# A retention head's key scaling, states and outputs moved 12 to 14 steps later behind the pair of products they come from

## The chip, the cores and the metric

One core of one Trainium2 chip runs the program. The metric is the device time of one execution in microseconds. The median of three runs before the change is 1666.28 us (1666.15 to 1666.56).

## What is computed

One layer of a streaming encoder over 512 frames of 2048 channels: a norm, one large projection, two mixers whose outputs are gated and merged, an output projection, and a gated addition. The change lies in mixer B, a retention of eight heads in chunks, cut here to its core:

```python
scores = einsum('bnqhd,bnkhd->bnhqk', qc, kc) * intra_decay
intra = einsum('bnhqk,bnkhe->bnqhe', scores, vc)
kv = einsum('bnkhd,bnkhe->nbhde', kc * to_end, vc)
def step(state, kv_c):
    return state * chunk_decay + kv_c, state
_, prev = lax.scan(step, zeros, kv)
cross = einsum('bnqhd,nbhde->bnqhe', qc * from_start, prev)
y = intra + cross      # then a GroupNorm per head
```

qc and kc are the rotated queries and keys of a head, vc its values. The kernel works in chunks of 128 frames, so a head has four blocks of queries and three states.

## The kernel before

All large products are written as pairs: `gemm_pair` (L255) makes two blocks of 128 output channels from seven products of half size (a Strassen scheme), in four PSUM banks p, v, q and r. Each weight is split into a high half wh, made on ACT (L156), and a low rest wl, made on DVE (L161); L163 and an accumulating transfer on POOL (L119) form the sums of weights. The seven products n = 0 to 6 are run in 14 runs of eight matmuls: 0h, 1h, 0l, 1l, 2h, 3h, 2l, 3l, 4l, 4h, 5h, 5l, 6l, 6h (h with wh, l with wl). They stand in the trace as L326, with the names ps_v for n = 0 and 5, ps_p for 1, 4 and 6, ps_q for 2 and ps_r for 3. After some runs results are taken out of PSUM: ACT copies one (L265), DVE combines two (L269, e_t) and adds halves (L1117, go).

The order of the instructions on each engine is written out by hand. `step()` is called after every second matmul of a pair, 56 times a pair, and advances a count. `later(n, f)` puts f in line to be recorded n steps on. What f does is then recorded at that place in the order of its engines, and each engine works through its own order; between engines there are semaphores.

The part around the change is the loop over the eight heads (L1130): for each head one pair that makes its queries and keys (`u_r`), then two pairs of gate channels (`u_g`). When a gate half is complete, `to` (L1124) makes its sigmoid on ACT (L1126, go<-go) and ACT issues its store (L1127). I call the two pairs behind a head's own its first and second gate pair; all of the head's further work is recorded between their matmuls.

That work is in `retention(h)` (L896). Queries and keys are rotated (`rotate`, L907). Counted from the rotation of the keys, which is one step into the first gate pair, a table (L1013 to L1017) says at which step each part is recorded:

- `queries` (L919): the queries times their factor, qt, on DVE.
- `keys(0)` to `keys(2)`: the keys are transposed in 32x32 blocks on DVE (kb, L940), sent to DRAM by four transfers (L948) and loaded back turned as kr (L958), all transfers on SP.
- `keys(3)`: ACT scales kr to kn (L961).
- `scores` and `decay`: ps_rs on PE (L928), at on DVE (L932).
- `states`: ps_kv on PE (L969, weights kn), then the states on ACT (L972) and DVE (L975).
- `values_out`: seven products ps_y on PE (L984, L986) from at, qt and the states.
- `norm`, `scale`, `back`: statistics, scaling and turning of the outputs on DVE and POOL (L991 to L1003, L940), sent to DRAM as yb.

Beside this a top-k step is recorded on DVE now and then (L776, L777, with rows of 256, 384 or 512 scores), one in each 40 steps, by a background queue.

Of the kernel before, what the change touches and what calls it, by code (L numbers as in the profile page):

```python
# [21 lines left out]
NT = L // 128  # L22
# [13 lines left out]
def block_kernel(tc, xT, pT, posb, posq, w_in, w_v, w_r0, w_r1, w_ik, w_a, w_b, w_o, w_ple, w_gate,  # L36
# [4 lines left out]
    with contextlib.ExitStack() as ctx:  # L41
# [10 lines left out]
        def U(name, dt=F32):  # L52
            return up.tile([128, L], dt, name=name, tag="u")

        def B(name, dt=F32):
            return bp.tile([128, 1280], dt, name=name, tag="b")

        def P(name):
            return pp.tile([128, L], F32, name=name, tag="p")

        def S(name, n):
            return sm.tile([128, n], F32, name=name, tag=f"s{n}")

        def tok(t):
            return slice(128 * t, 128 * t + 128)
# [381 lines left out]
        for k in range(KT):  # L447
            if k in (1, 2, 3, 4, 5, 7, 9, 11, 13, 15):
                load_to(state["raw"] + 1)
            if k < 10:  # L450
                t = U("xk")
                sp.dma_start(t, xT[:, k, :])
                xs.append(t)
            elif k % 2 == 0:
                t = B("xk2")
# [440 lines left out]
        def retention(h):  # L896
# [38 lines left out]
            def turn(src, n, name):  # L935


                b = U(name)
                w = 32 * n
                dve.transpose(out=b[:, 0:4 * w].rearrange("p (j t c) -> p t j c", j=4, t=n),  # L940
                              in_=src[:, 0:4 * w].rearrange("p (t j c) -> p t j c", t=n, j=4))
                return b[:, 0:4 * w]

            def send(b, dst):

                w = b.shape[1] // 4
                for i in range(4):
                    sp.dma_start(dst.rearrange("(j r) (i x) -> i r j x", j=4, i=4)[i],  # L948
                                 b[32 * i:32 * i + 32, :].rearrange("r (j x) -> r j x", j=4))

            def keys(i):
                if i == 0:
                    E["kb"] = turn(E[1], 3, "kb")
                elif i == 1:
                    send(E["kb"], krd[h])
                elif i == 2:
                    E["kr"] = U("kr")
                    sp.dma_start(E["kr"][:, 0:384], krd[h])  # L958
                else:
                    E["kn"] = U("kn")  # L960
                    act.activation(E["kn"][:, 0:384].rearrange("p (t i c) -> p i t c", t=3, i=4),  # L961
                                   E["kr"][:, 0:384].rearrange("p (i t c) -> p i t c", i=4, t=3),
                                   AF.Copy, scale=dect[:, 256:257])

            def states(i):
                if i == 0:
                    ps = E["ps"] = P("ps_kv")
                    for t in range(3):
                        pe.matmul(ps[:, tok(t)], E["kn"][:, tok(t)], rv[:, tok(t)], start=True, stop=True)  # L969
                elif i == 1:  # L970
                    E["s"] = U("state")
                    act.activation(E["s"][:, 0:128], E["ps"][:, 0:128], AF.Copy)  # L972
                else:
                    for t in (1, 2):
                        dve.scalar_tensor_tensor(E["s"][:, tok(t)], E["s"][:, tok(t - 1)], g128, E["ps"][:, tok(t)],  # L975
                                                 op0=OP.mult, op1=OP.add)

            def values_out(t):
                if t == 0:
                    E["py"] = P("ps_y")  # L980
                    E["st"] = S("gst", 24)
                    E["mv"] = S("gmv", 8)
                o = E["py"][:, tok(t)]
                pe.matmul(o, E["at"][:, tok(t)], rv[:, tok(t)], start=True, stop=(t == 0))  # L984
                if t:
                    pe.matmul(o, E["qt"][:, tok(t - 1)], E["s"][:, tok(t - 1)], start=False, stop=True)  # L986
# [20 lines left out]
            def back(i):  # L1007
                if i == 0:
                    E["yb"] = turn(E["yn"], NT, "yb")
                else:  # L1010
                    send(E["yb"], yd[h])

            steps = [(9, queries), (11, lambda: keys(0)), (21, lambda: keys(1)), (29, lambda: keys(2))]  # L1013
            steps += [(24, scores), (28, decay), (36, lambda: keys(3))]
            steps += [(n, lambda i=i: states(i)) for i, n in enumerate((41, 43, 45))]
            steps += [(53, lambda t=t: values_out(t)) for t in range(NT)]
            steps += [(59, norm), (70, scale), (74, lambda: back(0)), (84, lambda: back(1))]  # L1017
            return rotate

        x_wanted = collections.deque(x_away)  # L1020
# [109 lines left out]
        for h in range(NH):  # L1130
            if state["rate"] == BG_RATES[2]:
                later(38, lambda: hold(True))
                later(64, lambda: hold(False))
            gate_pair(u_r[h], retention(h))
            for n in (2 * h, 2 * h + 1):
                d, m = ((sgb, 2 * n), (sga, 2 * n - 16))[n >= 8]
                gate_pair(u_g[n], to(d[m:m + 2], AF.Sigmoid))
# [187 lines left out]
        for m in PAIRED:  # L1325
            t = B("sm")
# [18 lines left out]
        for m in range(8):  # L1345
# [13 lines left out]
            if m == 7:  # L1359
                todo.extend([None] * 24)  # L1360
                for k in range(2):
                    t = U("pk")
# [14 lines left out]
        for m in range(MF):  # L1377
            i = u_p[m // 4][0]
# [12 lines left out]
            t = U("pw")  # L1391
# [360 lines left out]
```

## Time and profile before

| what | value |
|---|---|
| median of three runs | 1666.28 us |
| the profiled execution's own time | 1665.03 us |
| its span, first to last instruction | 1663.2 us |
| PE (matmuls) busy | 1643.0 us, 99% of the span |
| DVE busy | 1313.7 us, 79% |
| ACT busy | 963.3 us, 58% |
| POOL busy | 233.0 us, 14% |
| chain that ended last | PE 87%, DVE 6%, ACT 3%, DMA 3%, issue 1% |

PE is matmuls, PEld the loading of their weights, SP the engine that issues most transfers. The retention heads run from about 280 to 770 us. In a timeline each line is a start, a duration, the engine, the line of the kernel, the operation, what it writes <- what it reads, the shape and a count; in brackets stands how long the engine had been idle before it and what released it. An engine's idle time costs something only where PE comes to wait for it. The matmuls are of 32-bit type and show as two instructions each where both halves of an operand are 32 bits wide (ps_kv: three products, six instructions).

### The profile page before, as it was taken

To read this page: it belongs to the slowest core of one execution; us is meant where nothing else is said; L and a number is where in the kernel's file an instruction comes from. 1 tells how busy PE (TensorE), PEld (TensorE's weight loads), DVE (VectorE), ACT (ScalarE), POOL (GpSimd) and SP (SyncE) were. 2 spreads that over 40 slices of the span, in tenths; PEclk is the share of its full clock that TensorE was granted. 3 is DMA by queue.
4 is the path that set the end of the run, shared out by engine and by line. 5 is a ranking of instruction groups with operands and counts; after the bars stand their busy time and mean duration, and the time that the engine had idled before them with its cause. 6 is when DMAs were issued, how large, how long until landed. Compare 5 with 4: busy or idle time off the path is not lost.

```text
span 1663.2 us, 25259 instructions
## 1 busy us (share of the span) xinstructions
PE 1643.0 (99%) x9278; PEld 1442.4 (87%) x9278; DVE 1313.7 (79%) x2038; ACT 963.3 (58%) x1481; POOL 233.0 (14%) x257
## 2 busy tenths in 40 slices
PE   9999999999999999999999999999999999999998
PEld 8988888888888888888888888888888888888997
DVE  8788879878988888877766766687768877888884
ACT  6556545555555555666877766566643544576653
POOL 3100111111111112112331122100000111100112
PEclk9999999999999999999999999999999999999999
DMA  8327999788788788788998888998566688765973
GB/s 314 111 87 238 325 258 270 191 215 220 194 217 222 193 207 222 175 229 240 254 245 223 214 231 219 241 370 283 184 206 193 182 213 220 207 218 149 245 229 143
DMA packets 138747, 365.84 MB, mean 220 GB/s; under 512 B 20672, under 2 KB 34496, under 8 KB 138624
## 3 DMA queue, kind: packets, MB, share of 16 engines
q1 hardware_dynamic: 98368, 242.92, 42.6%
q0 software_dynamic: 27440, 98.32, 31.7%
q10 hardware_dynamic: 12816, 23.00, 3.8%
q8 instruction: 73, 1.20, 0.3%
q14 instruction: 50, 0.41, 0.1%
HBM read 314.89 MB, written 49.28 MB: 219 GB/s over the span
## 4 chain that ended last, share of the span: by engine, by line
PE 87%; DVE 6%; ACT 3%; DMA 3%; issue 1%; SPq 0%; DVEq 0%; ACTq 0%
PE ps_p L326 23%; PE ps_v L326 15%; PE ps_q L326 8%; PE ps_r L326 7%; PE ps_w L233 3%; PE ps_w L232 3%; PE ps_w L234 3%; PE ps_vn L881 2%; PE ps_vn L880 2%; PE ps_vn L879 2%; DMA kr<-krd 2%; PE ps_iq L234 1%; PE ps_iq L232 1%; PE ps_iq L233 1%; DVE wl L161 1%
## 5 line engine op out<-in xcount | busy, mean ns | idle before, releaser
L161 DVE TENSOR_TENSOR wl<-wraw,wh 128x1024 fp32r<-128x1024 f32 (+3 forms) x472 | 568.1, 1216 | 160.1 <-ACT wh L156 158.1
L156 ACT ACTIVATE wh<-wraw 128x1024 fp32r<-128x1024 f32 (+3 forms) x471 | 485.9, 1041 | 241.8 <-DVE wraw L163 116.6
L119 POOL DMA_DIRECT2D wraw<-w_in x120 | 106.5, 963 | 583.6 <-DVE wl L161 343.0
L326 PE MATMUL ps_p<-hs,wh 128*128 128x512 f32 x640 | 162.4, 393 | 0.0
L265 ACT ACTIVATE e<-ps_p 128x512 f32<-128x512 f32 x152 | 90.2, 594 | 114.7 <-PE ps_p L326 113.9
L326 PEld LDWEIGHTS ps_p<-hs,wh 128*128 128x128 f32 x640 | 114.5, 189 | 19.9
L326 PE MATMUL ps_p<-hs,wl 128*128 128x256 f32 x640 | 90.2, 284 | 0.0
L326 PEld LDWEIGHTS ps_p<-hs,wl 128*128 128x128 f32 x640 | 82.5, 192 | 0.5
L326 PE MATMUL ps_v<-ha,wh 128*128 128x512 f32 x320 | 81.1, 392 | 0.0
L326 PE MATMUL ps_q<-ha,wh 128*128 128x512 f32 x320 | 80.7, 394 | 0.0
L326 PE MATMUL ps_v<-hs,wh 128*128 128x512 f32 x320 | 79.1, 389 | 0.0
L326 PE MATMUL ps_r<-hs,wh 128*128 128x512 f32 x320 | 79.0, 389 | 0.0
L326 PE MATMUL ps_p<-ha,wh 128*128 128x512 f32 x320 | 79.0, 389 | 0.0
L800 ACT ACTIVATE mk<-relf,thr 128x512 f16<-128x512 f32 (+3 forms) x128 | 66.6, 554 | 16.5 <-DVE go L1117 12.0
L1117 DVE TENSOR_TENSOR go<-e_t 128x256 f32<-128x256 f32 x160 | 68.2, 426 | 5.7
L326 PEld LDWEIGHTS ps_v<-hs,wh 128*128 128x128 f32 x320 | 60.1, 188 | 12.7
L326 PEld LDWEIGHTS ps_r<-hs,wh 128*128 128x128 f32 x320 | 60.1, 188 | 12.5
L326 PEld LDWEIGHTS ps_p<-ha,wh 128*128 128x128 f32 x320 | 60.1, 188 | 12.5
L119 POOL DMA_DIRECT2D wraw<-w_o x24 | 21.1, 942 | 348.5 <-DVE t L356 191.5
L326 PEld LDWEIGHTS ps_v<-ha,wh 128*128 128x128 f32 x320 | 59.5, 188 | 11.9
L269 DVE TENSOR_TENSOR e_t<-ps_p,pv 128x512 f32<-128x512 f32 x48 | 33.1, 690 | 46.0 <-ACT e L265 45.9
L326 PEld LDWEIGHTS ps_q<-ha,wh 128*128 128x128 f32 x320 | 57.5, 189 | 12.1 <-issue 1.7
(478 smaller groups left out, 3807.4 us busy)
## 6 DMA issues: line engine op xcount, KB each, us to landing
wraw<-w_in SPq DMA_DIRECT2D x170, 512.0 KB, 5.3
wraw<-w_in POOLq DMA_DIRECT2D x120, 512.0 KB, 8.0
wraw<-w_o SPq DMA_DIRECT2D x32, 512.0 KB, 5.0
wraw<-w_o POOLq DMA_DIRECT2D x24, 512.0 KB, 6.7
wraw<-w_gate SPq DMA_DIRECT2D x24, 512.0 KB, 5.1
wraw<-w_v SPq DMA_DIRECT2D x16, 512.0 KB, 9.2
wraw<-w_b SPq DMA_DIRECT2D x16, 512.0 KB, 5.7
wraw<-w_a SPq DMA_DIRECT2D x16, 512.0 KB, 4.2
```

What stands on the lines that cost most here:

```text
L119: pool.dma_start(out=view(raw_tiles[r], nk, cols), in_=src[:, k0:k0 + nk, :], accum_op=OP.add)
L156: act.activation(h, raw, AF.Copy)
L161: dve.tensor_sub(l, raw, h.bitcast(F32))
L232: pe.matmul(o, h[:, k, w], a, start=(s == order[0]), stop=False)
L233: pe.matmul(o, h[:, k, w], b, start=False, stop=False)
L234: pe.matmul(o, l[:, k, w], a, start=False, stop=(s == order[-1]))
L265: act.activation(E[n], src, AF.Copy)
L326: pe.matmul(o[:, co], w[:, k], src, start=(n < 4 and begin and k == 0 and j == 0), stop=(ended[n] == 16), skip_group_check=True)
L800: act.activation(bias_e[b][i // per][:, ln * (i % per):ln * (i % per + 1)], relf[:, :ln], AF.Sign, bias=thr[:, q:q + 1])
L879: pe.matmul(o, a[:, tok(t)], h[:, k], start=(s == 0), stop=False)
L880: pe.matmul(o, a[:, tok(t)], l[:, k], start=False, stop=False)
L1117: dve.tensor_add(o[:, q], c0, c1)
```

## The change

Only the table of steps is changed. `queries` goes from step 9 to 44, `keys(1)` from 21 to 20, `keys(2)` from 29 to 27, `keys(3)` from 36 to 50, the three `states` from 41, 43, 45 to 53, 55, 57, `values_out` from 53 to 66, `norm` from 59 to 72, `scale` from 70 to 83, `back` from 74 and 84 to 87 and 97. `keys(0)`, `scores` and `decay` stay. What is computed stays the same.

```diff
--- before.py
+++ after.py
@@ -1010,11 +1010,11 @@
                 else:
                     send(E["yb"], yd[h])
 
-            steps = [(9, queries), (11, lambda: keys(0)), (21, lambda: keys(1)), (29, lambda: keys(2))]
-            steps += [(24, scores), (28, decay), (36, lambda: keys(3))]
-            steps += [(n, lambda i=i: states(i)) for i, n in enumerate((41, 43, 45))]
-            steps += [(53, lambda t=t: values_out(t)) for t in range(NT)]
-            steps += [(59, norm), (70, scale), (74, lambda: back(0)), (84, lambda: back(1))]
+            steps = [(11, lambda: keys(0)), (20, lambda: keys(1)), (27, lambda: keys(2))]
+            steps += [(24, scores), (28, decay), (44, queries), (50, lambda: keys(3))]
+            steps += [(n, lambda i=i: states(i)) for i, n in enumerate((53, 55, 57))]
+            steps += [(66, lambda t=t: values_out(t)) for t in range(NT)]
+            steps += [(72, norm), (83, scale), (87, lambda: back(0)), (97, lambda: back(1))]
             return rotate
 
         x_wanted = collections.deque(x_away)
```

**ACT, the second head's first gate pair, before.** wh is the high half of a weight, e a copy out of PSUM, kn the scaled keys, go<-go a gate half's sigmoid, the DMA its store.

```order
L156 ACTIVATE wh<-wraw 128x1024 x3
L961 ACTIVATE kn<-kr,dect 128x4x3x32
L265 ACTIVATE e_3728<-ps_p 128x512
L156 ACTIVATE wh<-wraw 128x1024
L972 ACTIVATE state<-ps_kv 128x128
L156 ACTIVATE wh<-wraw 128x1024
L1126 ACTIVATE go<-go 128x512
L1127 DMA sgb<-go 128x512
```

The scaled keys come behind three wh, ahead of the copy e, of two more wh and of the sigmoid.

**ACT, the same place, after.**

```order
L156 ACTIVATE wh<-wraw 128x1024 x3
L265 ACTIVATE e_3724<-ps_p 128x512
L156 ACTIVATE wh<-wraw 128x1024 x2
L1126 ACTIVATE go<-go 128x512
L1127 DMA sgb<-go 128x512
L961 ACTIVATE kn<-kr,dect 128x4x3x32
L972 ACTIVATE state<-ps_kv 128x128
L265 ACTIVATE e_3783<-ps_p 128x512
```

kn has moved behind the copy, both wh, the sigmoid and the issue of its store; `state` now follows it directly.

**DVE, the same pair from the transposed keys on, before.** kb is the transposed keys, wl a weight's low rest, m and isc a top-k step, e_t and go<-e_t the taking out of a product.

```order
L921 TENSOR_TENSOR qt<-go,dect 128x384
L940 STREAM_TRANSPOSE kb<-go 128x3x4x32
L161 TENSOR_TENSOR wl<-wraw,wh 128x1024 x2
L163 TENSOR_TENSOR wraw<-wraw 128x1024
L269 TENSOR_TENSOR e_t<-ps_q,e_3640 128x512
L1117 TENSOR_TENSOR go<-e_t 128x256
L932 TENSOR_TENSOR at<-ps_rs,dect 128x512
...
L161 TENSOR_TENSOR wl<-wraw,wh 128x1024 x2
L975 SCALAR_TENSOR_TENSOR state<-state,ps_kv 128x128 x2
L269 TENSOR_TENSOR e_t<-ps_v,e_3728 128x512
L1117 TENSOR_TENSOR go<-e_t 128x256
```

qt stands right ahead of kb, and the two state updates right ahead of the e_t that reads ps_v.

**DVE, the same place, after.**

```order
L940 STREAM_TRANSPOSE kb<-go 128x3x4x32
...
L161 TENSOR_TENSOR wl<-wraw,wh 128x1024 x2
L921 TENSOR_TENSOR qt<-go,dect 128x384
L269 TENSOR_TENSOR e_t<-ps_v,e_3724 128x512
L1117 TENSOR_TENSOR go<-e_t 128x256
L161 TENSOR_TENSOR wl<-wraw,wh 128x1024
L269 TENSOR_TENSOR e_t<-ps_p,pv 128x512
L1117 TENSOR_TENSOR go<-e_t 128x256
L269 TENSOR_TENSOR e_t<-ps_r,e_3783 128x512
L1117 TENSOR_TENSOR go<-e_t 128x256
L161 TENSOR_TENSOR wl<-wraw,wh 128x1024
L975 SCALAR_TENSOR_TENSOR state<-state,ps_kv 128x128 x2
```

qt now stands between the last wl and that e_t; the state updates have gone behind the pair's last go and the next wl.

## Rows read from the trace of the kernel before

**Rows 1.** The page, part 4: the chain that ended last, by engine and line.
```profile
PE 87%; DVE 6%; ACT 3%; DMA 3%; issue 1%; SPq 0%; DVEq 0%; ACTq 0%
PE ps_p L326 23%; PE ps_v L326 15%; PE ps_q L326 8%; PE ps_r L326 7%; PE ps_w L233 3%; PE ps_w L232 3%; PE ps_w L234 3%; PE ps_vn L881 2%; PE ps_vn L880 2%; PE ps_vn L879 2%; DMA kr<-krd 2%; PE ps_iq L234 1%; PE ps_iq L232 1%; PE ps_iq L233 1%; DVE wl L161 1%
```

**Rows 2.** The waits: engine, line, what for; us in total, times, longest.
```profile
PEld ps_kv L969 <- ACT kn L961: 14.6, 8, 3.0
...
ACT kn L961 <- DMA kr<-krd: 12.6, 7, 2.6
...
PE ps_kv L969 <- ACT kn L961: 11.2, 7, 2.6
```

**Rows 3.** The timeline of the second head's first gate pair.
```profile
347.46 1.98 PE L326 MATMUL ps_v<-hs,wh 128*128 128x512 f32 x8
...
354.79 0.69 DVE L776 MAX8 m<-isc 128x8 f32<-128x512 f32 x1
...
356.19 0.55 DVE L921 TENSOR_TENSOR qt<-go,dect 128x384 f32<-128x384 f32 x1
...
356.65 0.57 DVE L940 STREAM_TRANSPOSE kb<-go 128x384 f32<-128x384 f32 x1
...
362.30 1.21 DVE L161 TENSOR_TENSOR wl<-wraw,wh 128x1024 fp32r<-128x1024 f32 x1
...
362.41 1.07 PE L326 MATMUL ps_v<-ha,wh 128*128 128x512 f32 x4
...
363.44 0.42 DVE L776 MAX8 m<-isc 128x8 f32<-128x256 f32 x1
...
364.29 1.22 DVE L161 TENSOR_TENSOR wl<-wraw,wh 128x1024 fp32r<-128x1024 f32 x1
...
365.41 0.61 ACT L961 ACTIVATE kn<-kr,dect 128x384 f32<-128x384 f32 x1 [2.56 <-DMA kr<-krd]
...
366.08 0.94 PE L969 MATMUL ps_kv<-rvh,kn 128*128 128x128 f32 x6 [2.60 <-ACT kn L961]
...
367.49 1.23 DVE L161 TENSOR_TENSOR wl<-wraw,wh 128x1024 fp32r<-128x1024 f32 x1 [1.98 <-ACT wh L156]
```

**Rows 4.** The timeline of PE, third head's first gate pair.
```profile
412.05 1.75 PE L326 MATMUL ps_v<-hs,wh 128*128 128x512 f32 x7
...
426.84 1.07 PE L326 MATMUL ps_v<-ha,wh 128*128 128x512 f32 x4
```

**Rows 5.** The timeline of a pair without retention work ahead of its end.
```profile
387.01 1.98 PE L326 MATMUL ps_v<-ha,wh 128*128 128x512 f32 x8
...
388.79 1.23 DVE L161 TENSOR_TENSOR wl<-wraw,wh 128x1024 fp32r<-128x1024 f32 x1 [0.35 <-ACT wh L156]
...
388.82 1.12 PE L326 MATMUL ps_v<-ha,wl 128*128 128x256 f32 x8
...
389.98 0.69 DVE L269 TENSOR_TENSOR e_t<-ps_v,e 128x512 f32<-128x512 f32 x1
...
390.74 2.00 PE L326 MATMUL ps_p<-hs,wh 128*128 128x512 f32 x8
...
391.16 0.63 ACT L1126 ACTIVATE go<-go 128x512 f32<-128x512 f32 x1 [1.08 <-DVE go L1117]
```

**Rows 6.** The timeline at the start of the second head's second gate pair.
```profile
373.09 1.99 PE L326 MATMUL ps_v<-hs,wh 128*128 128x512 f32 x8
...
373.93 0.69 DVE L269 TENSOR_TENSOR e_t<-ps_p,pv 128x512 f32<-128x512 f32 x1 [2.49 <-ACT e L265]
...
376.17 0.63 ACT L1126 ACTIVATE go<-go 128x512 f32<-128x512 f32 x1 [1.33 <-DVE go L1117]
...
377.26 1.06 ACT L156 ACTIVATE wh<-wraw 128x1024 fp32r<-128x1024 f32 x1 [0.46 <-ACT go L1126]
```

**Rows 7.** The tile qt: count, duration ns min/median/max, first and last start.
```profile
L921 DVE TENSOR_TENSOR qt<-go,dect x8: 546/549/552, 292.6 to 736.2; 128x384 f32<-128x384 f32 x8
```

**Rows 8.** The windows: busy us and count of PE, PEld, DVE, ACT, POOL, then clock, DMA.
```profile
275.00:760.00 485.00, 473.61 (x2787) 418.29 (x2786) 411.39 (x646) 267.70 (x348) 76.17 (x79) 1.00 0.83 211
```

## Prediction

> **What bounds the kernel now.** I read the page's chain first. PE carries 87% of it, and the one link that is not arithmetic and comes again and again is the load kr<-krd, 2% of the span [rows 1]. The waits say where PE stands still: past the start it is nearly all in one place, ps_kv (L969) waiting for kn (L961) on ACT, 11.2 us in seven of the eight heads as PE's matmuls count it and 14.6 us in eight as its weight loads do. Behind that stands ACT waiting for kr, 12.6 us [rows 2].
>
> The timeline of the second head's first gate pair (start 347.46) shows the mechanism. I name a pair's runs of eight matmuls by product and half: 4h, 5h (ps_v<-ha,wh at 362.41), 5l (the same product with wl), 6l, 6h (ps_p<-hs,wh). ACT comes to kn 2.56 us before kr has landed, starts it at 365.41, and ps_kv follows at 366.08, 0.67 later. A wh that is due on ACT stands behind kn, and DVE, which needs it, idles for 1.98 us until 367.49 [rows 3]. So the wait stops three engines, and DVE leaves it with nothing queued when 5l ends.
>
> What PE loses by pace: in this head 5h starts 14.95 us into the pair, in the third head 14.79 (426.84 less 412.05), the usual figure [rows 3, 4]. The 0.16 is a run held for a late wl; I count it with the loss. Half of 5h is 0.91 (half of 388.82 less 387.01, in a pair without retention, [rows 5]), so ps_kv was due at 15.70 and came at 18.62: 2.92 lost. Done so for the eight heads: 1.6, 2.9, 0.9, 0.4, 1.9, 2.1, 3.0, 0.7, together **13.4 us**, between the two figures of the waits. That is all the change can win.
>
> **The change, part by part.** *keys(3) from 36 to 50, states(0) from 41 to 53.* ps_kv moves from the middle of 5h to the middle of 6h, 3.73 us of matmuls (390.74 less 387.01, [rows 5]), and kn goes with it. kr lands 2.56 us after today's turn of kn, so the wait for kr is over. But kn now stands on ACT behind the sigmoid of the gate's first half and the issue of its store (L1126, L1127), in every head. That sigmoid waits for go (L1117) on DVE, that for e_t (L269), and that for the end of 5l on PE. A new chain ends at ps_kv, and PE comes to it soon after 5l.
>
> When PE gets there: 3.73 + 0.91 = 4.64 after the start of 5h, 19.43 into the pair.
>
> When kn is ready: e_t to the sigmoid takes 1.18 (389.98 to 391.16, [rows 5]); from a sigmoid to the next instruction behind its store 1.09 (376.17 to 377.26, [rows 6]); kn to ps_kv 0.67 [rows 3]. So ps_kv starts 2.94 after e_t does, and PE waits wherever e_t starts later than 16.49 into the pair. It can't start that early: 5l, which it reads, ends 2.93 after 5h starts (387.01 to the end of the run at 388.82), at 17.72 [rows 5].
>
> When e_t starts. Two things hold it. (a) ACT, which copies the end of 4h and then makes the wh for the last wl ahead of e_t: that wl starts 1.78 after 5h does (387.01 to 388.79, [rows 5]). A wl takes 1.14 to its successor (362.30 to 363.44), and qt, which the change puts right behind it, 0.46 (356.19 to 356.65, [rows 3]). So e_t is not before 14.79 + 1.78 + 1.14 + 0.46 = 18.17, and the wait not under **1.68 us** a head. (b) DVE itself. Its stream has no gap from kb to the wl at 364.29, and today's pause of 1.98 behind that goes, for the wh it waited on no longer stands behind kn. With qt gone from ahead of it, kb starts where qt does now, 356.19, and all of it moves 0.46 forward [rows 3]: wl at 363.83, the next at 364.97, qt 366.11, e_t 366.57. Sigmoid 367.75, kn 368.84, ps_kv **369.51**; PE is there at 347.46 + 19.43 = 366.89. It waits **2.6 us**, against 2.9 now.
>
> The same count for the other heads: from kb to e_t lie 9.53 us of DVE work (366.57 less 356.19, less 0.85 for the top-k step from 363.44 to 364.29) and whatever top-k step falls between; the longest takes 1.40 (354.79 to 356.19), the middle one 1.13 [rows 3]. kb would start at 8.45, 8.73, 8.18, 7.31, 8.18, 8.44, 9.15 and 7.31 into the pairs, which is where qt starts now: the first of the eight at 292.6 in a pair from 284.19, the last at 736.2 in one from 728.85 [rows 7]. With top-k steps of 1.40, 0.85, 1.13, 1.40, 1.13, 1.40, none, none this puts e_t at 19.4, 19.1, 18.8, 18.2, 19.3, 19.4, 19.1, 18.2; in the fifth head the step comes behind the wl that (a) holds, in the seventh ACT has a mask more to make, 0.9 late, in the eighth (a) alone decides. The waits are 2.9, 2.6, 2.3, 1.7, 2.8, 2.9, 2.5, 1.7, together **19.4 us**.
>
> *queries from 9 to 44.* Counted above: 0.46 earlier for kb, and so for kr, and 0.46 more ahead of e_t. Its reader is values_out, 22 steps later.
>
> *keys(1), keys(2) one and two steps earlier.* The rows of SP and of POOL stand in the same order before and after, so no transfer passes another. Zero; cover: kr is there at 365.41 now and wanted at 368.84.
>
> *values_out from 53 to 66.* The same matmuls, now in the next pair. They need the states, which DVE makes behind two e_t, two go and one wl of that pair. The first of these e_t starts 0.84 into a pair (373.09 to 373.93, [rows 6]), the five take about 3.3, the two state updates 0.6: ready near 4.8. PE reaches the first product at about 4.4 and the one that needs the second update some 1.2 later. Zero, with 0.8 of cover.
>
> *norm, scale, back 13 steps later.* No matmul of this stage reads them. The products leave the first gate pair and lengthen the second by about 1.5 us, so DVE gets room where it gets work. Zero.
>
> **The sum.** 19.4 - 13.4 = 6.0 us more. The profiled execution took 1665.03, so it would take 1671.0; the median shown is 1.25 above it: **1672.2 us**. Lower end: were DVE always free when 5l ends, e_t would start 0.04 behind it, as at 389.98; PE would be at ps_kv 1.67 later (391.65) and kn's product 2.94 later, so 1.27 a head and 10.1 in all [rows 5], 3.3 less than now: 1663.0. Upper end: if another 0.6 (the time of two state updates) gathered on DVE or ACT in each head, 4.8 more: 1677.0. I take the count by DVE's own stream, since its rows show no gap that could absorb it.
>
> **Rivals.** *DVE keeps up* (0.13). The point that decides is e_t's start, at or near the end of 5l. For it: in pairs without retention it is so [rows 5]. Against: those have no qt, kb or at ahead of it. 1663 to 1669, no change that can be told.
>
> *The wait is gone* (0.07): kr's landing was the whole of it, all 13.4 us come back, and the time is 1652.9, faster. It decides if kn is done 4.6 us after 5h starts. For it: before kn ACT waits for kr alone now [rows 2]. Against: kn's place on ACT behind the sigmoid, and that nothing ran past a waiting kn on ACT, the wh least of all [rows 3].
>
> *A second wait, at ps_y or for loads* (0.10). The cover of 0.8 above is thin, and the later store of yb holds SP's queue, behind which weight loads stand. With another 1 us a head the time is 1680.
>
> *The clock falls* (0.03). The granted clock is 1.00, the level of 2.4 GHz, over the whole stage [rows 8], waits of up to 3.0 us at the weight loads included [rows 2]; the longest that I forecast is no longer. If it fell, PE's work behind ps_kv to the end of the next pair's first run, about 3.4 us, would take twice as long in eight heads: 1699. The Trainium skill, "TensorE: Matmul & The Clock Gate", Part 1, says that a TensorE left idle goes back to 1.2 GHz; by that rule a stall that grows at this place costs more than itself. The trace so far shows no stall that did it.
>
> **How the numbers follow.** My forecast has 0.67. Runs of this kernel can tell 0.2%, 3.3 us, from no change. Slower by more: most of my own case (0.62), the second wait and the clock, 0.75. Within: the rest of mine and most of the first rival, 0.16. Faster: the wait gone and the lowest end of the first rival, 0.09. The range 1666.0 to 1678.0 holds my case, the upper part of the first rival and the nearer part of the second wait.
>
> **What would show it.** In the changed kernel's profile ACT's wait for kr at L961 should be gone, and L1126, waiting for go, should stand right ahead of kn in time; PE's wait at ps_kv should be 16 to 21 us by the pace, in the middle of 6h, with e_t (L269, reading ps_v) starting 18 to 19.5 us into each first gate pair; DVE's pause before the last wl should be gone. I am wrong if kn starts within 1 us of the end of 5l, or if e_t does.

## The result and the profile after

The changed kernel takes 1686.88 us, median of five runs (1684.96 to 1689.56), against 1666.28 before: ratio 1.0119, 95% interval 1.0101 to 1.0137. That is 20.6 us slower where 6 were forecast, and above the range. (The 1666.28 is also the median of five runs of the kernel before, which go from 1665.19 to 1670.87.)

In the profiled execution (1689.56 us, span 1687.4) the page's chain no longer helps: its shares add up to 61%, and the load kr<-krd of [rows 1] is not among its lines.

```profile
PE 54%; DVE 3%; ACT 2%; issue 1%; DMA 1%; DVEq 0%; ACTq 0%
```

So I go to the waits of the changed kernel, over the retention heads alone (280 to 780 us): engine, line, what for; us in total, times, longest.

```profile
ACT wh L156 <- DMA wraw<-w_in: 23.2, 16, 3.4
...
PE ps_kv L969 <- ACT kn L961: 19.0, 8, 3.3
...
ACT kn L961 <- ACT go L1126: 3.8, 8, 0.7
...
PEld ps_r L326 <- ACT wh L156: 3.3, 7, 1.2
...
PEld ps_p L326 <- DVE wl L161: 2.3, 4, 1.0
```

Three things are read here against [rows 2]. kn's wait for kr is gone, and in its place kn waits for the sigmoid L1126, in all eight heads. ps_kv waits for kn more than before, 19.0 against 11.2. And there are small waits of PE for weights, with ACT waiting 23.2 us for their loads; the same row before reads 3.5 (shown in experiment 2).

The timeline of the second head's first gate pair, which starts at 349.81, answers to [rows 3]:

```profile
369.65 0.55 DVE L921 TENSOR_TENSOR qt<-go,dect 128x384 f32<-128x384 f32 x1
...
370.12 0.68 DVE L269 TENSOR_TENSOR e_t<-ps_v,e 128x512 f32<-128x512 f32 x1
370.84 0.42 DVE L1117 TENSOR_TENSOR go<-e_t 128x256 f32<-128x256 f32 x1
...
371.30 0.63 ACT L1126 ACTIVATE go<-go 128x512 f32<-128x512 f32 x1 [2.72 <-DVE go L1117]
371.96 0.33 ACTq L1127 DMA_DIRECT2D sgb<-go  x1
372.39 0.61 ACT L961 ACTIVATE kn<-kr,dect 128x384 f32<-128x384 f32 x1 [0.46 <-ACT go L1126]
...
373.06 0.94 PE L969 MATMUL ps_kv<-rvh,kn 128*128 128x128 f32 x6 [2.19 <-ACT kn L961]
...
373.75 1.41 PE L326 MATMUL ps_p<-hs,wh 128*128 128x512 f32 x4
...
374.96 3.38 PE L326 MATMUL ps_v<-hs,wh 128*128 128x512 f32 x8
...
378.17 2.00 PE L326 MATMUL ps_p<-ha,wh 128*128 128x512 f32 x8
```

The chain is the forecast one: qt, e_t, go, the sigmoid, its store, kn, ps_kv, and 2.94 us from e_t (370.12) to ps_kv (373.06), to the hundredth. But the row at 374.96 is new: the eight matmuls of the next pair's first run take 3.38 us, where the same run takes 1.98 in [rows 3]. The windows show why (us of the window, busy us and count of PE, PEld, DVE, ACT, POOL, then the granted clock, DMA's share, GB/s):

```profile
371.00:374.50 3.50, 1.44 (x9) 1.34 (x10) 1.40 (x2) 1.52 (x3) 1.72 (x3) 1.00 0.83 178
374.50:377.92 3.42, 3.42 (x9) 2.67 (x8) 2.02 (x4) 1.55 (x2) 0.07 (x1) 0.50 0.95 202
377.92:381.33 3.41, 3.41 (x22) 3.02 (x21) 1.74 (x4) 1.69 (x2) 0.00 (x0) 1.00 1.04 211
...
275.00:780.00 505.00, 482.43 (x2759) 421.26 (x2759) 407.42 (x634) 266.88 (x345) 75.07 (x78) 0.98 0.79 201
```

From 374.50 to 377.92 the granted clock is 0.50, the 1.2 GHz level, and PE gets 9 instructions done where the next stretch of the same length, with shorter matmuls among its own, holds 22. Such a stretch, 3.41 us long each time, follows the wait at ps_kv in six of the eight heads: at 306.24, 374.50, 439.36, 572.48, 640.74 and 709.01. The profiled execution before has none ahead of the last 5 us. [Rows 8] said 1.00 over the stage; now it is 0.98.

**Where the 24.2 us between the two spans went** (1687.4 less 1663.2):

- The wait at ps_kv by the pace: 2.8, 2.4, 2.4, 2.0, 3.0, 3.4, 2.4, 1.9 in the eight heads, 20.3 together against 13.4: 6.9.
- Late weights: PE comes later to the middle of 6h in the first gate pairs, by 5.7 us in the eight together, and three of the heads' own pairs take 20.69, 20.72 and 19.93 instead of 19.64 (from a pair's first matmul to the end of its last), 2.4: together 8.1.
- That leaves 9.2 for the six stretches at half the clock, of which each can cost up to 1.7 (half of 3.41). The rows agree. From ps_kv to the next pair's second run it is 5.11 us in the second head (373.06 to 378.17) and 3.54 in the fourth, where the clock stays at 1.00:

```profile
505.37 0.94 PE L969 MATMUL ps_kv<-rvh,kn 128*128 128x128 f32 x6 [1.88 <-ACT kn L961]
...
508.91 1.98 PE L326 MATMUL ps_p<-ha,wh 128*128 128x512 f32 x8
```

Over the heads it is 5.05 to 5.12 in the six with such a stretch and 3.54 to 3.55 in the other two: 1.6 for each fall, 9.4 for six.

### The profile page after: what moved, and what is told of

It reads as the page before. It is cut to its first block, busy times and chain, and to the rows that moved or that the text cites. A ratio compares the mean times of both kernels' runs of the same rounds, so it can differ in the third digit from the quotient of the medians.

```text
span 1687.4 us, 25266 instructions
## 1 busy us (share of the span) xinstructions
PE 1656.0 (98%) x9278; PEld 1448.9 (86%) x9278; DVE 1313.3 (78%) x2038; ACT 964.4 (57%) x1481; POOL 233.4 (14%) x257
## 4 chain that ended last, share of the span: by engine, by line
PE 54%; DVE 3%; ACT 2%; issue 1%; DMA 1%; DVEq 0%; ACTq 0%
PE ps_p L326 16%; PE ps_v L326 10%; PE ps_q L326 5%; PE ps_r L326 5%; PE ps_w L232 3%; PE ps_w L233 3%; PE ps_w L234 3%; PE ps_pg L234 1%; PE ps_pg L232 1%; PE ps_pg L233 1%; DMA wraw<-w_in 1%; PE ps_pg L1536 1%; PE ps_pg L1538 1%; PE ps_pg L1537 1%; PE ps_bias L813 1%
## 5 line engine op out<-in xcount | busy, mean ns | idle before, releaser
L119 POOL DMA_DIRECT2D wraw<-w_in x120 | 106.1, 945 | 563.4 <-DVE wl L161 424.7
L326 PE MATMUL ps_v<-hs,wh 128*128 128x512 f32 x320 | 84.7, 410 | 0.0
L326 PEld LDWEIGHTS ps_v<-hs,wh 128*128 128x128 f32 x320 | 65.0, 203 | 14.5
L119 POOL DMA_DIRECT2D wraw<-w_o x24 | 21.1, 939 | 348.6 <-DVE t L356 191.5
```

The lines of the kernel that those rows point to most:

```text
L119: pool.dma_start(out=view(raw_tiles[r], nk, cols), in_=src[:, k0:k0 + nk, :], accum_op=OP.add)
L326: pe.matmul(o[:, co], w[:, k], src, start=(n < 4 and begin and k == 0 and j == 0), stop=(ended[n] == 16), skip_group_check=True)
```

## The experiments

My theory then: three separate costs, the wait at ps_kv, falls of the clock that this idle time of PE brings, and weights that come late because yb's store holds SP's queue. The main rivals: the falls have a cause of their own; the weights are late because DVE and ACT have more to do. All times are medians; each run's kernel before was measured beside it, and its median was 1668.16, 1670.33 and 1668.19 in the three groups (experiments 1 to 4, 5 to 7, 8 and 9). The changed kernel was not measured again beside them, so "less than the changed kernel" compares across groups. Counted from each group's own kernel before, the same gains are 2 to 4 us larger: 28.9, 10.2, 9.1, 36.1 and 10.7 in experiments 1, 2, 3, 4 and 6.

**1. The keys' scaling ahead of the sigmoid.**

```diff
-            steps += [(24, scores), (28, decay), (44, queries), (50, lambda: keys(3))]
+            steps += [(24, scores), (28, decay), (44, queries), (45, lambda: keys(3))]
```

> The changed kernel with one part altered: keys(3) at step 45, so that kn stands on ACT between the last two wh of the pair, ahead of the sigmoid (L1126) and its store; states stay in the middle of 6h. Theory (kn's place behind the sigmoid makes the wait at ps_kv, and the idle PE there makes the clock fall): the 20 us of wait by pace go nearly to zero, no stretch of granted clock 0.5 after ps_kv, so 10 us of falls go too; the late weights stay (about 7 us): 1660, at most 1664. Rival A (the falls have another cause than the wait): the falls stay, about 1667 to 1670. Rival B (kr lands so late that kn waits again, now holding a wh): a wait for kr of over 1 us a head at kn, 1670 or more.

Measured: 1659.89 us (1658.65 to 1661.87), ratio to before 0.9949 (0.9930 to 0.9967), 27.0 less than the changed kernel. The same place of its timeline, in the pair that starts at 345.32:

```profile
364.44 0.62 ACT L961 ACTIVATE kn<-kr,dect 128x384 f32<-128x384 f32 x1 [1.51 <-DMA kr<-krd]
...
365.69 0.68 DVE L269 TENSOR_TENSOR e_t<-ps_v,e 128x512 f32<-128x512 f32 x1
...
366.27 0.83 PE L969 MATMUL ps_kv<-rvh,kn 128*128 128x128 f32 x6
...
366.87 0.63 ACT L1126 ACTIVATE go<-go 128x512 f32<-128x512 f32 x1 [0.86 <-DVE go L1117]
```

ps_kv has no bracket: PE does not wait. kn still waits 1.51 for kr, in four heads 4.0 us together, and PE has work all the while. No stretch at 0.50 is left ahead of the kernel's last 5 us. The wait and the falls go together, which excludes rival A; the late weights stay (PE's weight loads wait 3.8 us for wh at ps_r).

**2. The store of yb behind the loads.**

```diff
-            steps += [(72, norm), (83, scale), (87, lambda: back(0)), (97, lambda: back(1))]
+            steps += [(72, norm), (83, scale), (87, lambda: back(0)), (112, lambda: back(1))]
```

> The changed kernel with one part altered: back(1), with the store of yb, at step 112 instead of 97, so that on SP's queue the store stands behind the loads of the next weights. Theory (the store, which becomes ready later than before at the same place of SP's queue, holds the loads of wraw behind it; so wh and wl come late): SP's wait for yb falls from 57 us to under 25, PE's small waits for wh and wl (some 5 us at ps_r, ps_p, ps_v) shrink below 1.5, own pairs of a head take 19.7 again instead of 20.7; time 1679 to 1682. Waits at ps_kv and the clock's falls stay. Rival (weights are late because DVE and ACT have more to do there, not for SP): no change, 1685 to 1689, and the time from landing to wh grows instead.

Measured: 1678.57 us (1677.33 to 1680.46), ratio 1.0062 (1.0041 to 1.0083), 8.3 less than the changed kernel. back(1) is the four stores and nothing else; on SP one load of wraw moves ahead of them. The rows of SP, POOL and ACT around the own pair of the fifth head show what that does. The kernel before, pair from 517.18:

```profile
509.66 1.78 SPq L948 DMA_DIRECT2D yd<-yb  x4
511.48 1.81 SPq L132 DMA_DIRECT2D wraw<-w_in  x3
...
515.60 0.92 POOL L119 DMA_DIRECT2D wraw<-w_in  x1 [10.39 <-DVE wl L161]
...
523.44 1.06 ACT L156 ACTIVATE wh<-wraw 128x1024 fp32r<-128x1024 f32 x1
```

The changed kernel, pair from 528.13:

```profile
522.58 1.78 SPq L948 DMA_DIRECT2D yd<-yb  x4
524.40 1.41 SPq L132 DMA_DIRECT2D wraw<-w_in  x3
...
526.33 0.92 POOL L119 DMA_DIRECT2D wraw<-w_in  x1 [8.23 <-DVE wl L161]
...
537.35 1.06 ACT L156 ACTIVATE wh<-wraw 128x1024 fp32r<-128x1024 f32 x1 [2.88 <-DMA wraw<-w_in]
...
539.72 1.21 PE L326 MATMUL ps_p<-hs,wl 128*128 128x256 f32 x8 [0.33 <-DVE wl L161]
```

This experiment, pair from 521.73:

```profile
508.35 4.07 SPq L132 DMA_DIRECT2D wraw<-w_in  x2
516.18 1.77 SPq L948 DMA_DIRECT2D yd<-yb  x4
518.05 0.88 SPq L132 DMA_DIRECT2D wraw<-w_in  x2
...
519.93 0.92 POOL L119 DMA_DIRECT2D wraw<-w_in  x1 [8.23 <-DVE wl L161]
...
529.14 1.06 ACT L156 ACTIVATE wh<-wraw 128x1024 fp32r<-128x1024 f32 x1 [1.07 <-DMA wraw<-w_in]
```

Counted from the start of the pair, the stores came at -7.52 before and at -5.55 after, and the three loads behind them at -5.70 and -3.73. The third wh of the pair came at 6.26 before and at 9.22 after, where ACT waits 2.88 us for a load. With one load let ahead of the stores it comes at 7.41, and the pair takes 19.64 again.

The transfer that this wh waits for is none of SP's three. It is POOL's accumulating one (L119), the row between, which is issued no later than before: 1.58 us ahead of the pair before, 1.80 ahead in both kernels after. It takes longer to land, and wh starts when it lands. In KB and us from issue to landing, before, in the changed kernel and here:

```profile
wraw<-w_in POOLq DMA_DIRECT2D x1, 512.0 KB, 7.8
```
```profile
wraw<-w_in POOLq DMA_DIRECT2D x1, 512.0 KB, 11.0
```
```profile
wraw<-w_in POOLq DMA_DIRECT2D x1, 512.0 KB, 9.2
```

In the seven own pairs of the stage the first of these transfers has medians of 8.4, 10.5 and 9.2, and in the changed kernel 14 of the 16 waits, 22.3 of the 23.2 us, end with one of POOL. So the loads behind the store, issued 2 us later, come close ahead of POOL's transfer: the first of them 4.12 us ahead of it before, 1.93 in the changed kernel with three loads, 1.88 here with two. While POOL's transfer is in flight the DMA share is 1.02, 1.01 and 0.99, so that it shares full engines with them fits; no run moves POOL's transfers alone. The totals of the stage agree. Before, the changed kernel and this one:

```profile
ACT wh L156 <- DMA wraw<-w_in: 3.5, 5, 1.2
...
SPq L948 <- DVE yb L940: 28.0, 6, 5.1
```
```profile
SPq L948 <- DVE yb L940: 57.1, 7, 8.9
```
```profile
ACT wh L156 <- DMA wraw<-w_in: 8.7, 8, 2.4
...
SPq L948 <- DVE yb L940: 32.9, 8, 5.1
```

The wait for yb was to fall under 25 and is 32.9: the two kernels after are 57.1 and 32.9, in the expected direction, and PE's small waits, as its weight loads count them, go from 8.4 to 1.5. The time is 0.4 under the expected range. The falls were to stay, and the profiled execution has three instead of six; but the four runs' mean clock, 0.993 to 0.996, is that of the changed kernel's five, 0.992 to 0.996, so the falls don't explain the 8.3. DVE's and ACT's work was left where it was, so in the changed kernel most of it is the store's place. What is left of the late weights lies in the sixth and seventh heads, where PE comes to 6h 0.4 and 1.2 late and kb starts 1.0 and 1.1 later than counted.

This run also tests the count of the wait without the late weights. e_t starts 19.34, 19.09, 18.81, 18.34, 19.31, 20.38, 20.10 and 18.18 us into the eight first gate pairs, within 0.15 of the forecast in six of them, and the waits at ps_kv are 19.4 together by the pace, as forecast.

**3. Fill for the idle time.**

```diff
                     ps = E["ps"] = P("ps_kv")
+                    for n in range(6):
+                        pe.matmul(ps, identr, Xh["s3"][0], start=True, stop=True)
```

> The changed kernel with six more matmuls of 128x512 in each head, written into ps_kv's own bank right ahead of its three products and overwritten by them: 1.4 us of PE work a head into a wait of 1.9 to 3.4 us. Theory (PE standing still at ps_kv is what makes the clock fall): the wait left at ps_kv is 0.5 to 2 us a head, the six falls go, nothing else moves: 1676 to 1680, about 8 less although PE has 11 us more to do. Rival A (the clock falls for another reason, such as the load of the chip over the whole stage): falls stay in five or six heads, time 1685 to 1689. Rival B (the fills delay ps_kv since the wait is not real slack): 1690 to 1698.

Measured: 1679.66 us (1677.48 to 1681.71), ratio 1.0067 (1.0046 to 1.0088): 7.2 less than the changed kernel, with 48 matmuls more to do. The waits, and the only stretch at 0.50 in the stage with the stretch ahead of it:

```profile
PE ps_kv L971 <- ACT kn L961: 7.8, 8, 1.9
```
```profile
629.75:633.16 3.42, 1.55 (x9) 1.03 (x8) 2.07 (x3) 1.24 (x2) 1.62 (x3) 1.00 0.64 114
633.16:636.58 3.42, 3.42 (x11) 2.74 (x10) 0.63 (x1) 1.53 (x3) 0.85 (x1) 0.50 1.06 239
```

ps_kv's idle time goes from 19.0 to 7.8 us, the falls from six to one, and the mean granted clock of the runs from 0.992 to 0.996 up to 0.997 to 0.999. The load of the chip was not lowered, the idle time was. Rivals A and B are both out. The remaining fall is in the sixth head, which had the longest wait. Between the two profiled executions, each the slowest of its kernel's runs, lie 7.9 us and five falls: again 1.6 each, if nothing else differs.

**4. Both alterations, 1 and 2.**

> The changed kernel with both alterations: keys(3) at 45 and back(1) at 112. Theory (wait at ps_kv with the falls, and late weights by SP's queue, are the two causes and independent): 1653 to 1658, faster than the kernel before by 8 or more, PE waits in the eight heads under 5 us together. Rival (they share a cause, so the two gains don't add): 1660 or more.

Measured: 1652.71 us (1652.32 to 1654.12), ratio 0.9907 (0.9888 to 0.9927): faster than the kernel before by 15 us. The gains of 1 and 2 add nearly: 27.0 and 8.3 make 35.3, measured 34.2 (from the group's own kernel before, 39.1 and 36.1). The time is 0.3 under the expected range. There is no fall in the stage, and the chain on its page is PE again:

```profile
PE 95%; DVE 3%; ACT 1%; issue 0%; DMA 0%; DVEq 0%; ACTq 0%; SPq 0%
```

**5. The later tail alone, in the kernel before.**

```diff
-            steps += [(59, norm), (70, scale), (74, lambda: back(0)), (84, lambda: back(1))]
+            steps += [(72, norm), (83, scale), (87, lambda: back(0)), (97, lambda: back(1))]
```

> The kernel before with one part of the change alone: norm, scale, back(0) and back(1) 13 steps later; all else as before. Theory (the later tail alone makes yb ready later at its old place on SP's queue, and so the weights late): SP's wait for yb 50 us or more against 28, new waits of PE for wh and wl of 3 to 6 us, kn's wait for kr and ps_kv's wait as before; 4 to 7 us more than the kernel before of the same runs. Rival (the late weights need the new places of kn, ps_kv or the products as well): within 2 us of the kernel before.

Measured: 1684.45 us (1678.58 to 1687.14), ratio 1.0071 (1.0045 to 1.0097), so 7.5 to 16.2 us slower. Its waits in the stage:

```profile
PEld ps_r L326 <- ACT wh L156: 5.2, 6, 1.5
...
PEld ps_p L326 <- DVE wl L161: 4.3, 7, 1.0
```
```profile
SPq L948 <- DVE yb L940: 56.8, 7, 8.8
```

The direction and SP's wait are as expected, the size is twice that: the profiled execution, which has no fall in the stage, takes 1678.58 against 1665.03. Of these 13.5 us the own pairs hold 4.6 and the first gate pairs 9.2 (205.7 together against 196.5; the second gate pairs and what lies around change little). So a step that I costed at zero is by itself worth more than the whole change was forecast to cost.

**6. The queries' factor behind e_t.**

```diff
-            steps += [(24, scores), (28, decay), (44, queries), (50, lambda: keys(3))]
+            steps += [(24, scores), (28, decay), (50, lambda: keys(3)), (56, queries)]
```

> The changed kernel with one part altered: queries recorded at step 56 instead of 44, so that qt stands on DVE behind the pair's last takings-out instead of right ahead of e_t. Theory (DVE's own stream sets when e_t starts): e_t 0.46 us earlier in each first gate pair that DVE binds, kn and ps_kv with it, so 2.5 to 3.7 us less wait at ps_kv in eight heads and at most as many falls of the clock: 1680 to 1685. Rival (e_t is held by the end of 5l or by ACT, DVE keeps up): no change, 1686 to 1688. Second rival (qt comes too late for ps_y): new waits at ps_y, over 1688.

Measured: 1680.24 us (1678.65 to 1681.62), ratio 1.0053 (1.0036 to 1.0071), 6.6 less than the changed kernel. In the second head, pair from 347.60:

```profile
367.49 0.68 DVE L269 TENSOR_TENSOR e_t<-ps_v,e 128x512 f32<-128x512 f32 x1
...
370.50 0.94 PE L969 MATMUL ps_kv<-rvh,kn 128*128 128x128 f32 x6 [1.80 <-ACT kn L961]
```

e_t starts 19.89 us into the pair instead of 20.31, 0.42 earlier for a qt that takes 0.46 on DVE; in the eighth head alone it does not come earlier. ps_kv's wait in the stage falls from 19.0 to 15.3, one fall is left of six, and nothing waits at ps_y for qt. So DVE's own stream does set e_t, and the rival "DVE keeps up" is out.

**7. Fill and later store together.** The edits are those of 2 and 3.

> The changed kernel with two alterations: six more matmuls of 128x512 ahead of ps_kv in each head (1.4 us of PE work in the wait, overwritten) and back(1) at step 112. Theory (the change costs three things: the wait at ps_kv, the falls it brings, and the late weights): with the second and third taken away and the wait left as fill plus rest, the time is what the wait alone costs, 1670 to 1673. Rival (falls are not from the wait, or the two alterations share a cause): 1676 or more.

Measured: 1672.60 us (1671.58 to 1674.47, ten runs), ratio 1.0014 (1.0004 to 1.0024). The median is 6.3 above the 1666.28 of the kernel before, and 2.3 above that of its own group, whose runs of the kernel before were granted 0.994 to 0.998; six of the ten runs here had 0.999. With the falls and the late weights mostly taken away, what stays of the change is about the term that I had forecast.

**8. Tail and store, in the kernel before.** The edit of 5 with back(1) at 112 instead of 97.

> The kernel before with norm, scale and back(0) 13 steps later, as in the change, and back(1) at step 112. Against the run in which the tail alone was moved (12 us more than the kernel before) only the place of yb's four stores on SP differs. Theory (what the later tail costs is the store that holds SP's queue): SP's wait for yb under 35 us, own pairs of a head at 19.7, time within 2 us of the kernel before of the same runs. Rival (DVE's later statistics and scaling make the weights late themselves): 8 us or more above the kernel before.

Measured: 1674.79 us (1672.07 to 1676.07), ratio 1.0038 (1.0025 to 1.0051), 6.6 above its kernel before: neither within 2 nor over 8. SP's wait for yb is 32.9, as in experiment 2. Its waits in the stage:

```profile
ACT kn L961 <- DMA kr<-krd: 14.5, 7, 3.5
PE ps_kv L969 <- ACT kn L961: 13.9, 7, 2.6
```

The own pairs are at 19.64 again in six of seven, so the store explains them and about half of what the tail costs. The rest lies in the first gate pairs, 203.9 us together against 196.5. Not all of that is the tail: one fall (eighth head, 751.17) is in it, and the profiled execution of experiment 9, the same program as before, takes 200.0 there, also with one fall. Against that one kb starts later in the third and seventh heads (9.80 us into the pair against 8.64, 11.02 against 9.64), and in the seventh ps_kv comes 1.4 later with it; in the sixth it does not (9.93 against 10.05). That the tail's work on DVE pushes kb fits this; it was not tried alone, and what holds the eighth head stays open. In the changed kernel kr is not waited for, so there it can show only as what experiment 2 leaves in the sixth and seventh heads.

**9. The store's step alone, in the kernel before.**

```diff
-            steps += [(59, norm), (70, scale), (74, lambda: back(0)), (84, lambda: back(1))]
+            steps += [(59, norm), (70, scale), (74, lambda: back(0)), (97, lambda: back(1))]
```

> The kernel before with back(1), the four stores of yb, at step 97 instead of 84, and nothing else moved. Theory (the store costs only while it waits for yb; place alone is free): SP's wait for yb falls from 28 us to under 15, time within 2 us of the kernel before of the same runs, or up to 3 less. Rival (step 97 is a bad place for four stores whatever they wait for): 5 us or more above it.

Measured: 1669.97 us (1663.32 to 1672.13, ten runs), ratio 1.0006 (0.9994 to 1.0019); SP's wait for yb is 28.0, as before. The expected fall to under 15 was an error of mine: SP gets no other transfer between steps 84 and 97, so every queue stands in the same order and the program is the kernel before again. It tells nothing on the store, but it shows how far one program's runs spread here: from 1663.32 at a mean clock of 0.999 to 1672.13 at 0.996. Its profiled execution has a fall of its own: behind a wait of 2.24 us at ps_kv (301.70, first head) the granted clock is 0.50 from 302.30 to 305.71. So the kernel before can fall in the same place.

## Why the prediction was wrong

**The wait for kr goes, one behind the sigmoid comes: right.** kn stands behind L1126 and L1127, 2.94 us lie between e_t and ps_kv as counted, DVE's stream sets e_t (experiment 6), and the waits are 20.3 us by the pace where 19.4 were forecast. (The 1.13 of the middle top-k step is not in [rows 3]; it stands at 291.51 of the same trace.) In the changed kernel that agreement is partly luck: e_t comes 18.37 to 20.84 us into the pairs, outside the stated 18 to 19.5 in five heads, and PE, held by late weights, comes late too. With most of the late weights gone, in experiment 2, both the starts of e_t and the sum are as counted. Experiment 7, with the two other costs mostly out of the way, comes to 1672.60; that this is the forecast median is again partly chance, for its own kernel before was 4 us slower than 1666.28.

**"norm, scale, back 13 steps later ... Zero": the step that failed first.** It cost 8.1 us in the changed kernel's stage. The cover that I named was that no matmul of this stage reads them, and that DVE gets room. I had also found SP's rows in the same order, and took the same order for the same timing. It is not. A transfer at its old place in a queue, ready 2 us later, moves everything behind it by 2 us: here three loads of weights, which then come close ahead of POOL's accumulating transfer, and that one lands 11.0 instead of 7.8 us after its issue (experiment 2). The tail alone costs 14.1 us by the medians in the kernel before (experiment 5), and giving the store a later place returns 8.3 in the changed one (experiment 2). The rival "a second wait" named this store, in half a sentence, with 1 us a head, which is the 8 measured. I gave it 0.10.

**"The clock falls (0.03)": the second.** I argued that waits of 2.9 and 3.0 us had been passed in the kernel before with the clock at 1.00, and that the new ones were no longer. The longest new one is 3.4 by the pace (sixth head), and the argument rested on one execution. Others of the same program were granted less: in the runs beside the experiments the kernel before took 1664.69 us at a mean clock of 0.999 and up to 1674.13 at 0.994. With a wait of 1.9 us or more in all eight heads instead of in four, six of them fall in the profiled execution. In the five runs of the changed kernel the time follows the clock, 1684.96 at 0.996 to 1689.56 at 0.992. For the fall I had priced 27 us (3.4 in each of eight heads). By the windows a stretch of 3.41 at half the clock can't cost over 1.7, and by the rows each costs 1.6. The Trainium skill, "TensorE: Matmul & The Clock Gate", Part 1, has an idle TensorE go back to 1.2 GHz; experiment 3 and the windows above agree with that, at granted 0.50 behind the waits at ps_kv.

**Queries: right in the sum, for the reason given.** At step 44 qt costs what it saves; at 56 it is off the path, and 6.6 us come back, more than the 3.7 of waits; its profiled execution has one fall instead of six, which fits.

**values_out: right.** In the changed kernel's stage PE has no wait at ps_y.

**The range.** The two costs that I put in rivals at 0.10 and 0.03 came together. For the profiled execution the forecast was 1671.0; 0.9 more of wait, 8.1 of late weights and 9.4 of falls make 1689.4, and it took 1689.56. The median run, at a mean clock of 0.995 and not 0.992, had fewer falls: about three, an estimate from the clock, since half of 3.41 is 0.1% of the span. I had treated the two as alternatives to my case, though both add to it.

## What to carry to other kernels

A queue with the same order is not a queue with the same timing: for each step that becomes ready later, look at what stands behind its transfer in the issuing queue, when that is due, and which other engine's transfers it will then be in flight with. Before moving a wait, ask what else the stalled engine's queue holds; here the keys' scaling had to go one place ahead of the sigmoid, at step 45 and not 50, and the store behind a load, and the same change is then worth 15 us the other way. Whether a stall lowers the clock is not to be read from one execution: take the granted clock of all runs.

## What was not expected of the hardware

- A wait of PE of 2.4 us by the pace (the second head) was followed by 3.41 us at a granted clock of 0.50, while the two waits of 2.9 and 3.0 in the profiled execution before were not. Which of them are followed by it differs from run to run: the same program ranges from 0.994 to 0.999 in its mean clock, and over 9 us in time.
- More work can take less time: 48 matmuls written into an idle bank, 1.57 us a head in the trace and so 12.6 in all, made the kernel 7.2 us shorter.
- Where a wait for a load ends need not be where the delay began. POOL's transfer of 512 KB at one place took 7.8, 11.0 and 9.2 us to land, with the DMA share at 0.99 to 1.02 each time, according to when SP's loads were let go.
